# Three pads ahead of and between the operands of TensorE's dense products, in a diffusion layer on one core

## The chip, the cores and the metric

The kernel runs on one core of one Trainium2 chip. Its time is the device time of one execution in microseconds (us); the median of several runs counts. Matrix products run on TensorE (PE), elementwise work on VectorE (DVE) and ScalarE (ACT), a little on GpSimd (POOL); SyncE (SP) issues most of the DMAs. The on-chip memory (SBUF) has 128 partitions. A tile takes a stretch of bytes, the same in every partition, and what this document calls its place or offset is where that stretch begins.

## The reference

One layer of a diffusion backbone over 256 latent tokens and 256 context tokens of width 2048, in float32:

```
h  = modulate(rmsnorm(x), shift, scale)       # also for the context tokens
rw, cv, z, ab, gt = split(h @ w_in)           # one wide input projection
o_a = two-way RWKV-7 scan over heads of rw
o_b = two-way chunked gated DeltaNet of cv, z, ab
m  = sigmoid(g_a) * (o_a @ p_a) + sigmoid(g_b) * (o_b @ p_b)
x  = x + gate1 * (m @ w_out)
f  = modulate(rmsnorm(x), shift2, scale2)
g, u = split(f @ w_gate_up)
x  = x + gate2 * ((silu(g) * u) @ w_down)
out = rmsnorm(x)
```

The FFN's hidden width is 5632. Shifts, scales and gates come from products of the condition vector with w_ada.

## The kernel before, in words

Activations lie with channels on partitions: a tensor of 2048 channels is 16 slices of [128, 256 tokens]. Every dense product is made of three matmuls per slice of 128 input channels. Weights and activations are split into a high part (a copy in the type float32r, made on ScalarE) and a low part (the rest, subtracted on VectorE), and `gemm` (lines 365 to 371) adds hi·hi, hi·lo and lo·hi into one bank of PSUM. The first operand of each matmul is the weights, 128 columns of 512 bytes; the second, the moving operand, is 256 columns (1024 bytes) or 512 (2048 bytes).

The weights come in chunks of up to 8 slices: a DMA loads `wraw` (three buffers), then `whi` and `wlo` (two buffers each) are filled from it. Three places do this: `load_w` (line 340) for the products after the mixers, `low_split` (line 487) for the first stage, and `cast` (line 1025) for the input projection. All of these tiles are in the pool `wp`. `low_split` puts only the even slices there, the odd ones into the pool `p0`.

The work runs in this order.

- To about 130 us: norms, the first part of w_ada, and the low-rank columns of the input projection, in an order written out by hand.
- To about 1390 us: the input projection (moving operands `hxh`, `hxl`, called hx) woven with the two mixers. Here a small planner (`Weave`) gives out the order of TensorE, VectorE, ScalarE and GpSimd by estimated costs. All instructions of this stage go through line 143.
- To about 1490 us: p_a and p_b with the moving operands `oah`, `oal` (oa).
- To about 1590 us: w_out with `mh`, `ml` (m), while the first weights of the FFN are put into a tile of their own, `W4` (its slices are called w in the profile).
- Then the FFN: w_gate_up with `hfh`, `hfl` (hf), and w_down with `za` (the first 32 slices of 128 hidden channels) and `zb` (the last 12).

In the last three steps the order comes from the framework's own schedule, with some instructions held in program order.

Pools are laid from both ends of a partition. From the left: `cst` (constants), `wp` (weights), the pool `arp` with the arena, then the mixers' pool, and in its place later those of m, hf and zb. From the right end: the pool of hx, later those of oa and of W4 and za (`hx`, `gp`, `zap`). Tiles take multiples of 32 bytes.

Of the kernel before, what the change touches and what calls it, by code (L numbers as in the profile page):

```python
# [11 lines left out]
F32 = mybir.dt.float32  # L12
F32R = mybir.dt.float32r
# [5 lines left out]
P = 128  # L19
# [249 lines left out]
def emit(ctx: ExitStack, tc, A, out, dbg=None):  # L269
    nc = tc.nc  # L270
    V, S, G, Q = nc.vector, nc.scalar, nc.gpsimd, nc.sync
# [6 lines left out]
    ent = ctx.enter_context  # L278

    cst = ent(tc.tile_pool(name="cst", bufs=1))  # L280
    wp = ent(tc.tile_pool(name="wp", bufs=2))
    pmm = ent(tc.tile_pool(name="pmm", bufs=3, space=PSUM))
    pa = ent(tc.tile_pool(name="pa", bufs=2, space=PSUM))
    pi = ent(tc.tile_pool(name="pi", bufs=1, space=PSUM))
# [49 lines left out]
    V.memset(scanm.rearrange("p (c t) -> p c t", t=64)[:, :, 0:1], 0.0)  # L334


    wpool, wbufs = [wp], [3, 2, 2]
    wstep = [4]

    def load_w(src, M, nk, kchunk=8, ks=0, into=None):  # L340

        res = []
        pieces = -(-(nk - ks) // kchunk)
        ends = [ks + (nk - ks) * (i + 1) // pieces for i in range(pieces)]
        for k0, k1 in zip([ks] + ends, ends):
            n = k1 - k0
            if into is None:
                raw = wpool[0].tile([P, 8, P], F32, tag="wraw", name="wraw", bufs=wbufs[0])
                hi = wpool[0].tile([P, 8, P], F32R, tag="whi", name="whi", bufs=wbufs[1])
                lo = wpool[0].tile([P, 8, P], F32R, tag="wlo", name="wlo", bufs=wbufs[2])  # L350
            else:
                raw = into[2].tile([P, 8, P], F32, tag="wr", name="wr")
                hi, lo = (t[:, k0:k1] for t in into[:2])
            ld = Q.dma_start(raw[:, :n, :M], src[:, k0:k0 + n, :])
            if into is not None:
                tc.keep_in_program_order(ld)
            for i in range(0, n, wstep[0]):
                c = slice(i, min(i + wstep[0], n))
                S.copy(hi[:, c, :M], raw[:, c, :M])  # L359
                V.tensor_sub(lo[:, c, :M], raw[:, c, :M], hi[:, c, :M].bitcast(F32))  # L360
            for k in range(n):
                res.append((k0 + k, hi[:, k, :M], lo[:, k, :M]))
        return res
# [44 lines left out]
    with tc.tile_pool(name="p0", bufs=1) as p0, \  # L408
# [14 lines left out]
        NL = 736  # L423
# [63 lines left out]
        def low_split(e):  # L487
            res = []
            for k in range(2):
                pool = p0 if e % 2 else wp  # L490
                hi, lo = (pool.tile([P, 8, P] if pool is wp else [P, NL], F32R, tag=f"{t}{k}" if pool is p0 else t, name=t,
                                    bufs=1 if pool is p0 else 2) for t in ("whi", "wlo"))
                if pool is wp:
                    hi, lo = (t.rearrange("p k m -> p (k m)")[:, :NL] for t in (hi, lo))
                S.copy(hi, lws[e][k])
                V.tensor_sub(lo, lws[e][k], hi.bitcast(F32))
                res.append((hi, lo))
            return res
# [10 lines left out]
        for part in range(NE + 1):  # L509
            if part < NE:  # L510
                ps = pst(pmm, "mm")
            for c in range(4):
                if part + 1 < NE:
                    load_ada(part + 1, c)
                if part < NE:
                    ada_part(ps, part, c)
                if c == 0 and part < NE:
                    w = low_split(part)
                    if part + 1 < NE:
                        load_low(part + 1)  # L520
                for _ in itertools.islice(before or (), (0, 1, 2, 1)[c]):
                    pass
            if part < NE:
                rows_of(part, ps, before or ())
                before = low_products(part, w)
            else:
                for _ in before:
                    pass
# [496 lines left out]
    def cast(src, i):  # L1025

        raws = []
        for c in range(2):
            raw = wp.tile([P, 8, P], F32, tag="wraw", name="wraw", bufs=3)
            raws.append((raw, weave.now + dq(raw, src[:, 8 * c:8 * c + 8, :])))  # L1030
        for c, (raw, at) in enumerate(raws):
            if i:
                yield "read", i - 1, c
            yield max(0.0, at - weave.now)
            hi, lo = (wp.tile([P, 8, P], F32R, tag=t, name=t) for t in ("whi", "wlo"))
            for k in range(0, 8, LAT['cg']):
                g = slice(k, k + LAT['cg'])
                yield s.copy(hi[:, g], raw[:, g])
                yield v.tensor_sub(lo[:, g], raw[:, g], hi[:, g].bitcast(F32))
                casts[i, 8 * c + k] = hi, lo  # L1040
                weave.ready("cast", i, 8 * c + k)
# [3 lines left out]
    def products():  # L1045
# [24 lines left out]
        while todo or nxt:  # L1070
            if nxt is None:
                nxt = choose()
                if nxt is None:
                    yield 0.5
                    continue
                if nxt[0] == "g":
                    nxt = "g", next(gate_next)
                weave.add(LAT['crank'], cast(source(*nxt), i))
            what, p = nxt
            nxt = choose()  # L1080
            if nxt is not None:
                if nxt[0] == "g":
                    nxt = "g", next(gate_next)
                weave.add(LAT['crank'], cast(source(*nxt), i + 1))
# [421 lines left out]
    for j in range(KT):  # L1506
        ps = pst(pmm, "mm")
        gemm(ps[:, 0:T], load_w(A["pa"][j], P, 8), Oa, T)
        S.copy(PA[:, j], ps[:, 0:T])
        tc.keep_in_program_order(S.activation(gts[:, 2 * j:2 * j + 2, :], gts[:, 2 * j:2 * j + 2, :], AF.Sigmoid))  # L1510
# [13 lines left out]
    for j in range(KT):  # L1524
        ps = pst(pmm, "mm")
        gemm(ps[:, 0:T], load_w(A["pb"][j], P, 8), Oa, T)
        G.tensor_mul(PA[:, j], PA[:, j], gts[:, j])
        m = x1p.tile([P, T], F32, tag="m", name="m")
        V.tensor_mul(m, ps[:, 0:T], gts[:, 16 + j])
        V.tensor_add(m, m, PA[:, j])  # L1530
        split(M[0][:, j], M[1][:, j], m)
# [6 lines left out]
    for j in range(KT):  # L1538
        ps = pst(pmm, "mm")
        gemm(ps[:, 0:T], load_w(A["wout"][j], P, KT), M, T)  # L1540
        V.scalar_tensor_tensor(x1[:, j, :], ps[:, 0:T], mod[:, 32 + j:33 + j], x1[:, j, :], ALU.mult, ALU.add)
        sq = square_sum(x1p, x1[:, j, :], ssum, j == 0)
        if 0 < j < KT - 1:
            V.tensor_add(ssum, ssum, sq)
        if j % 3 == 2 and j < 12:
            w4.append(load_w(A["wgu"][j // 3], P, KT, into=[W4[:, i, j // 3] for i in range(2)] + [zap]))
# [162 lines left out]
```

## Time and profile before

| | |
|---|---|
| median of 3 runs | 2342.61 us (2338.29 to 2344.66) |
| span of the profiled execution (its first to its last instruction) | 2342.3 us |
| mean granted TensorE clock | 0.972 |
| TensorE busy | 2200.5 us, 94% |
| VectorE busy | 1555.0 us, 66% |
| ScalarE busy | 1101.7 us, 47% |
| moved by DMA | 430.77 MB, mean 184 GB/s |

The profile has no other time of the profiled execution than its span. A group row of the profile reads: line, engine, operation, tile written <- tiles read, shape, count | busy us, mean ns of one | idle time before it and what ended that. A timeline row begins with the start and the length in us. A stage row has the stage, its length, the busy time and count of PE, weight loads (PEld), DVE, ACT and POOL, then the granted clock, the share of the DMA engines and GB/s. The length of a matmul is modelled and overlaps that of the next one, so the pace of a row of matmuls is read from their starts.

### The profile page before, as it was taken

Reading aid. Unit: us, or ns where it says so; the run is one execution under the profiler, and the core shown is the slowest. Engines: PE = TensorE matmul, PEld = TensorE weight load, DVE = VectorE, ACT = ScalarE, POOL = GpSimd, SP = SyncE. Lnnn points to the kernel's source line nnn. Section 1 sums busy time; section 2 is a strip of 40 time slices with the busy share of each in tenths; the row PEclk is TensorE's granted clock in tenths of the full one; section 3 lists DMA queues with packets and bytes.
Section 4 is the critical chain, followed back from the end, with each engine's and each line's share of the span. In section 5 each row is a group of like instructions: output and inputs, shape, how many; then the busy total and the mean of one; then the engine's idle time right before and its main releaser. Section 6 shows DMA issues by size and latency. Waiting matters only on the chain.

```text
span 2342.3 us, 54751 instructions
## 1 busy us (share of the span) xinstructions
PE 2200.5 (94%) x22904; PEld 1940.9 (83%) x22904; DVE 1555.0 (66%) x3238; ACT 1101.7 (47%) x2058; POOL 110.6 (5%) x183
## 2 busy tenths in 40 slices
PE   7989999999999999888888999999999999999998
PEld 4767677787777778666677989999999999999997
DVE  3447588888877568889788745765565655555554
ACT  3246454454455555454455546544444444444443
POOL 0000000000000011111111003000000000000000
PEclk9999999999999899989899999999999999999999
DMA  9956543443443237556566665563777766556665
GB/s 380 397 149 187 159 113 96 118 116 97 112 117 109 89 125 229 176 175 193 160 199 212 194 220 189 205 219 117 234 233 232 237 236 215 188 189 191 192 192 164
DMA packets 232727, 430.77 MB, mean 184 GB/s; under 512 B 114848, under 2 KB 130208, under 8 KB 228128
## 3 DMA queue, kind: packets, MB, share of 16 engines
q1 hardware_dynamic: 204832, 351.77, 47.3%
q0 software_dynamic: 13824, 50.34, 6.8%
q10 hardware_dynamic: 13824, 25.17, 3.3%
q8 instruction: 179, 2.93, 0.5%
q14 instruction: 68, 0.56, 0.1%
HBM read 401.44 MB, written 25.77 MB: 182 GB/s over the span
## 4 chain that ended last, share of the span: by engine, by line
PE 62%; DVE 11%; DMA 6%; ACT 4%; issue 2%; SPq 0%; ACTq 0%; DVEq 0%
PE mm L143 16%; PE mm L371 12%; PE mm L369 12%; PE mm L370 12%; PE s L143 4%; DVE arena L143 4%; PE pa L143 3%; PE pi L143 2%; DVE aw L143 2%; DVE wlo L143 2%; DMA wr<-wgu 1%; DMA tscr<-arena 1%; ACT arena L143 1%; DMA Tx<-tscr 1%; DVE wlo L360 1%
## 5 line engine op out<-in xcount | busy, mean ns | idle before, releaser
L360 DVE TENSOR_TENSOR wlo<-wraw,whi 128x1024 fp32r<-128x1024 f32 x328 | 393.0, 1199 | 348.8 <-ACT whi L359 345.7
L359 ACT CAST whi<-wraw 128x1024 fp32r<-128x1024 f32 x328 | 337.6, 1030 | 472.2 <-PE mm L370 427.9
L143 PE MATMUL mm<-hxh,wlo 128*128 128x256 f32 (+1 forms) x1376 | 471.0, 342 | 11.7 <-DVE wlo L143 11.3
L143 PE MATMUL mm<-hxh,whi 128*128 128x256 f32 (+1 forms) x1376 | 470.8, 342 | 8.7 <-ACT whi L143 7.3
L143 PE MATMUL mm<-hxl,whi 128*128 128x256 f32 (+1 forms) x1376 | 464.7, 338 | 0.0
L371 PE MATMUL mm<-hfh,wlo 128*128 128x256 f32 x1344 | 376.6, 280 | 0.6 <-DVE wlo L360 0.6
L369 PE MATMUL mm<-hfh,whi 128*128 128x256 f32 x1344 | 375.8, 280 | 0.0
L370 PE MATMUL mm<-hfl,whi 128*128 128x256 f32 x1344 | 374.7, 279 | 0.0
L143 PEld LDWEIGHTS mm<-hxh,wlo 128*128 128x128 f32 x1376 | 266.1, 193 | 42.4 <-DVE wlo L143 16.4
L143 PEld LDWEIGHTS mm<-hxh,whi 128*128 128x128 f32 x1376 | 266.8, 194 | 36.2 <-ACT whi L143 10.8
L143 PEld LDWEIGHTS mm<-hxl,whi 128*128 128x128 f32 x1376 | 266.5, 194 | 26.3 <-issue 5.7
L143 DVE TENSOR_TENSOR wlo<-wraw,whi 128x512 fp32r<-128x512 f32 x344 | 236.0, 690 | 68.3 <-ACT whi L143 66.7
L371 PEld LDWEIGHTS mm<-hfh,wlo 128*128 128x128 f32 x1344 | 252.6, 188 | 1.1 <-DVE wlo L360 1.0
L369 PEld LDWEIGHTS mm<-hfh,whi 128*128 128x128 f32 x1344 | 252.8, 188 | 0.0
L370 PEld LDWEIGHTS mm<-hfl,whi 128*128 128x128 f32 x1344 | 252.8, 188 | 0.0
L143 ACT CAST whi<-wraw 128x512 fp32r<-128x512 f32 x344 | 205.8, 617 | 98.7 <-PE mm L143 63.0
L369 PE MATMUL mm<-za,whi 128*128 128x256 f32 x512 | 141.6, 277 | 0.0
L371 PE MATMUL mm<-za,wlo 128*128 128x256 f32 x512 | 141.4, 276 | 0.0
L370 PE MATMUL mm<-za,whi 128*128 128x256 f32 x512 | 141.4, 276 | 0.0
L143 DVE TENSOR_TENSOR arena<-arena 128x39 f32<-128x39 f32 (+17 forms) x522 | 120.9, 234 | 23.8 <-DMA arena<-scr 8.0
L143 DVE SCALAR_TENSOR_TENSOR aw<-aw,ck 128x512 f32<-128x512 f32 x180 | 132.6, 750 | 6.0 <-DMA aw<-ada_rest 5.8
L370 PEld LDWEIGHTS mm<-za,whi 128*128 128x128 f32 x512 | 96.1, 188 | 0.0
(329 smaller groups left out, 3926.5 us busy)
## 6 DMA issues: line engine op xcount, KB each, us to landing
wraw<-w SPq DMA_DIRECT2D x172, 512.0 KB, 4.0
wraw<-wgu SPq DMA_DIRECT2D x168, 512.0 KB, 4.4
aw<-ada_rest POOLq DMA_DIRECT2D x96, 512.0 KB, 4.6
aw<-ada_first SPq DMA_DIRECT2D x32, 1024.0 KB, 11.7
wraw<-wdn SPq DMA_DIRECT2D x64, 448.0 KB, 3.5
wraw<-wout SPq DMA_DIRECT2D x32, 512.0 KB, 4.2
aw<-ada_gt ACTq DMA_DIRECT2D x64, 256.0 KB, 4.8
wraw<-wdn SPq DMA_DIRECT2D x32, 512.0 KB, 3.5
```

The source lines that it names most:

```text
L143: return Op(self, cost, lambda: getattr(self.engine, name)(out, *a, **k), split)
L359: S.copy(hi[:, c, :M], raw[:, c, :M])
L360: V.tensor_sub(lo[:, c, :M], raw[:, c, :M], hi[:, c, :M].bitcast(F32))
L369: E.matmul(ps, hi, Xh[:, k, :n], start=first and i == 0, stop=False)
L370: E.matmul(ps, hi, Xl[:, k, :n], start=False, stop=False)
L371: E.matmul(ps, lo, Xh[:, k, :n], start=False, stop=last and i == len(wt) - 1)
```

## The change

Three pads are added; no operation on data is changed. A tile `rpad` of 32 bytes is laid at the right end, ahead of the pools there. A tile `lpad` of 32 bytes is laid in `cst` after `scanm` (a mask), and so ahead of a few small constants and of `wp`. The tiles `whi` and `wlo` of `wp` get 16 numbers (64 bytes) behind their 8 slices, by a new helper that all three places call. Two small fills on VectorE write the first two pads.

```
@@ emit
     wp = ent(tc.tile_pool(name="wp", bufs=2))
+    rpad = ent(tc.tile_pool(name="rpad", bufs=1, side="right")).tile([P, 8], F32, name="rpad")
...
     V.memset(scanm.rearrange("p (c t) -> p c t", t=64)[:, :, 0:1], 0.0)
+    lpad = cst.tile([P, 8], F32, name="lpad")
+    V.memset(lpad, 0.0)
+    V.memset(rpad, 0.0)
+    def split_tile(tag, bufs=2):
+        return wp.tile([P, 8 * P + 16], F32R, tag=tag, name=tag, bufs=bufs)[:, :8 * P].rearrange("p (k m) -> p k m", k=8)
@@ load_w
-                hi = wpool[0].tile([P, 8, P], F32R, tag="whi", name="whi", bufs=wbufs[1])
-                lo = wpool[0].tile([P, 8, P], F32R, tag="wlo", name="wlo", bufs=wbufs[2])
+                hi, lo = split_tile("whi"), split_tile("wlo")
@@ low_split
-                hi, lo = (pool.tile([P, 8, P] if pool is wp else [P, NL], F32R, tag=f"{t}{k}" if pool is p0 else t, name=t,
-                                    bufs=1 if pool is p0 else 2) for t in ("whi", "wlo"))
-                if pool is wp:
-                    hi, lo = (t.rearrange("p k m -> p (k m)")[:, :NL] for t in (hi, lo))
+                hi, lo = (split_tile(t).rearrange("p k m -> p (k m)")[:, :NL] if pool is wp else
+                          p0.tile([P, NL], F32R, tag=f"{t}{k}", name=t) for t in ("whi", "wlo"))
@@ cast
-            hi, lo = (wp.tile([P, 8, P], F32R, tag=t, name=t) for t in ("whi", "wlo"))
+            hi, lo = (split_tile(t) for t in ("whi", "wlo"))
```

## The prediction

> **What bounds the kernel now.** I read the page's busy shares and its clock row first, then the chain that ended last, then the busy time by stage, then the groups of matmuls by form, and at last the starts of single matmuls. The first view shows TensorE (PE) busy for 94% of the span, far above the next engine; the chain names dense products (lines 369 to 371, and the "mm" products of line 143) for half of the path; the stages show where nothing but their pace counts.
>
> ```profile
> span 2342.3 us, 54751 instructions
> PE 2200.5 (94%) x22904; PEld 1940.9 (83%) x22904; DVE 1555.0 (66%) x3238; ACT 1101.7 (47%) x2058; POOL 110.6 (5%) x183
> by line: PE mm L143 16.1%; PE mm L371 12.2%; PE mm L369 12.1%; PE mm L370 12.1%; PE s L143 4.1%; DVE arena L143 3.9%; PE pa L143 3.2%; issue 2.1%; PE pi L143 2.1%; DVE aw L143 1.9%; DVE wlo L143 1.7%; DMA wr<-wgu 1.1%; DMA tscr<-arena 1.1%;
> 0.00:130.00 130.00, 113.56 (x1338) 81.07 (x1339) 54.27 (x147) 37.56 (x71) 0.41 (x5) 0.97 0.96 365
> 130.00:1390.00 1260.00, 1157.76 (x13691) 936.00 (x13690) 965.25 (x2378) 636.01 (x1432) 88.84 (x162) 0.96 0.51 150
> 1620.00:2087.00 467.00, 466.40 (x3980) 465.91 (x3979) 270.69 (x380) 198.52 (x248) 0.00 (x0) 1.00 0.66 221
> 2088.00:2325.00 237.00, 237.00 (x2071) 236.78 (x2070) 119.38 (x125) 106.27 (x127) 0.00 (x0) 1.00 0.64 190
> ```
>
> From 1620 us on PE never idles at a granted clock of 1.00, while VectorE is busy for 58% and the DMA engines for 64 to 66%. There a nanosecond per matmul is a nanosecond of the result. From 130 to 1390 us only part counts. The first 130 us are DMA-bound (share 0.96).
>
> The counts of the terms are those of the groups:
>
> ```profile
> L371 PE MATMUL mm<-hfh,wlo 128*128 128x256 f32 x1344 | 376.6, 280 | 0.6 <-DVE wlo L360 0.6
> L143 PE MATMUL mm<-hxl,whi 128*128 128x256 f32 x880 | 255.1, 290 | 0.0
> L143 PE MATMUL mm<-hxl,whi 128*128 128x512 f32 x496 | 209.6, 423 | 0.0
> L370 PE MATMUL mm<-za,whi 128*128 128x256 f32 x512 | 141.4, 276 | 0.0
> L371 PE MATMUL mm<-oah,wlo 128*128 128x256 f32 x256 | 71.9, 284 | 0.5 <-DVE wlo L360 0.5
> L371 PE MATMUL mm<-mh,wlo 128*128 128x256 f32 x256 | 72.7, 284 | 4.0 <-DVE wlo L360 4.0
> L371 PE MATMUL mm<-zb,wlo 128*128 128x256 f32 x192 | 53.8, 280 | 0.0
> ```
>
> Each row is one of three equal groups (hi·hi, hi·lo, lo·hi). Their "mean" is a modelled length, so the pace has to be taken from starts. These rows of the timeline are the first and the last of undisturbed stretches:
>
> ```profile
> 2105.11 0.28 PE L370 MATMUL mm<-za,whi 128*128 128x256 f32 x1
> 2111.91 0.28 PE L370 MATMUL mm<-za,whi 128*128 128x256 f32 x1
> ...
> 1430.02 0.28 PE L371 MATMUL mm<-oah,wlo 128*128 128x256 f32 x1
> 1437.09 0.28 PE L371 MATMUL mm<-oah,wlo 128*128 128x256 f32 x1
> ...
> 1655.01 0.28 PE L369 MATMUL mm<-hfh,whi 128*128 128x256 f32 x1
> 1690.01 0.28 PE L369 MATMUL mm<-hfh,whi 128*128 128x256 f32 x1
> 1850.03 0.28 PE L371 MATMUL mm<-hfh,wlo 128*128 128x256 f32 x1
> 1885.36 0.28 PE L371 MATMUL mm<-hfh,wlo 128*128 128x256 f32 x1
> ...
> 177.71 0.28 PE L143 MATMUL mm<-hxh,whi 128*128 128x256 f32 x1
> 180.21 0.28 PE L143 MATMUL mm<-hxl,whi 128*128 128x256 f32 x1
> 146.05 0.28 PE L143 MATMUL mm<-hxh,wlo 128*128 128x256 f32 x1
> 148.53 0.28 PE L143 MATMUL mm<-hxh,wlo 128*128 128x256 f32 x1
> ...
> 153.91 0.39 PE L143 MATMUL mm<-hxh,whi 128*128 128x512 f32 x1
> 159.18 0.39 PE L143 MATMUL mm<-hxh,wlo 128*128 128x512 f32 x1
> ```
>
> Start to start, at full clock and with the same shape: za 6.80 us over 60 matmuls, 113.3 ns; oa 7.07 over 60, 117.8; hf 35.00 over 300, 116.7, and after a stall at 1772 us 35.33 over 300, 117.8; hx 2.50 over 22, 113.6, but 2.48 over 21, 118, in most of its stretches (216 of some 1,700 undisturbed triples of starts are fast, hence a mean of 117.2). At 512 columns 5.27 over 23, 229. So the same product has several steady paces, 4% apart, which hold for tens of microseconds and change at a stall.
>
> Do places decide? I worked the byte offset of each tile in a partition out of the tile sizes, in the order in which the pools lay them, and took it modulo 128. The slices that a matmul reads are 512 or 1024 bytes apart, so one number tells a whole product. Before: the weights whi, wlo 32, all four buffers; the right-hand operands (hx, oa, za) 96; the left-hand ones (hf, m, zb) 64. The right-hand ones show a constant 113.3 or 117.8; the left-hand ones 116.7 or 117.8 and no 113.3. So place matters, but it is no full cause: oa and za share their offsets and differ by 4.5 ns.
>
> **The change part by part.** rpad takes 32 bytes at the right end: hx, oa, za go from 96 to 64. lpad takes 32 bytes ahead of the weights, and each of the four whi/wlo buffers grows by 64: the weights go from 32 to 64 (buffer 0) and 0 (buffer 1), which alternate by chunk of up to 8 slices. Everything laid after them moves by 32+4·64 = 288: hf, m, zb go from 64 to 96, the arena from 32 to 64.
>
> The two fills (memset) run on VectorE at the start, before it waits 3 us for a load; a fill of 8 numbers cost 65 ns, so they are hidden, and 0.13 us without that cover.
>
> ```profile
> L334 DVE MEMSET scanm<- 128x8 bf16 x1 | 0.1, 65 | 0.1
> 4.57 0.18 DVE L325 TENSOR_SCALAR om<-PR 128x29 f32<-128x29 f32 x1 [3.01 <-DMA PR<-prm]
> L496 DVE TENSOR_TENSOR wlo<-wraw,whi x16: 914/916/925, 29.1 to 114.3; 128x736 fp32r<-128x736 f32 x16
> L495 ACT CAST whi<-wraw x16: 787/800/806, 28.3 to 113.1; 128x736 fp32r<-128x736 f32 x16
> ```
>
> VectorE and ScalarE: in the first stage even slices are split into tiles at 32 and odd ones at 64, and the 16 splits lie within 914 to 925 and 787 to 806 ns. I take nothing; 1% either way stays beside PE. No DMA is added or moved in a queue, and no wait is added; wraw moves from 32 to 64, the first stage's aw from 64 to 96. No row prices an offset for DMAs, and I take 0 between -1 and +1 us in the DMA-bound first stage; later they have a third of their time in hand.
>
> That leaves the pace of TensorE. The row nearest to the new left-hand pairing (weights 64, moving 96) is an odd slice of the first stage:
>
> ```profile
> 131.92 0.28 PE L369 MATMUL pa<-hxh,whi 128*128 128x256 f32 x1
> 132.51 0.28 PE L371 MATMUL pa<-hxh,wlo 128*128 128x256 f32 x1
> 1598.49 0.28 PE L371 MATMUL mm<-hfh,w 128*128 128x256 f32 x1
> 1609.26 0.28 PE L369 MATMUL mm<-hfh,w 128*128 128x256 f32 x1
> 1593.01 0.41 PE L369 MATMUL mm<-hfh,whi 128*128 128x256 f32 x1
> 1593.87 0.41 PE L370 MATMUL mm<-hfl,w 128*128 128x256 f32 x1
> ```
>
> 0.59 us over 5 matmuls, 118.2 ns. Steps in us:
> - hf, m, zb, 3·(1344+256+192) = 5376 matmuls, 117.1 now (the two hf rows by their time; 192 matmuls with w are left out). Chunks with weights at 64: +1.1·2688 = +3.0. Chunks with weights at 0: no row; ends 113.3 (-10.2) and 118.2 (+3.0). Nearest by offset is again 118.2, but it comes from five matmuls without a settled cycle; I take the fast end, as a bet: -10.2. Together -7.2.
> - oa, 768: weights and moving now both start on a multiple of 64 bytes, where a slice spans 8 and 16 pieces of 64 bytes and not 9 and 17. Ends 0 and -4.45·0.768 = -3.4; I take -3.4.
> - za, 1536: stays at 113.3, 0; the other end is oa's pace, +6.8.
> - hx, 256 columns, 2640: 117.2 to 113.3 is -10.3, at 512 columns, 1488: some 230.7 (the mean over undisturbed starts) to 229 is -2.5. Of this stage's dense time, 2640·0.117+1488·0.231 = 653 us, the chain holds 16.1%, 377 us, so 0.58 of it counts: -7.4.
> Sum -18.0, from 2342.3 to 2324.3. The span is 0.3 us under the median of the runs, 2342.6, so no correction is made. Late next, as PE gets faster, is the split's write of wlo; its waits in the left-hand rows above are under 1 us in 1344, so it keeps up.
>
> [...]
>
> **The rivals.**
> - Only the relation of weights to moving operand counts, and modulo 64 it is the same before and after (0 on the right, 32 on the left). Then the same paces are drawn anew. For it: oa and za. Against it: the w4 rows below. Price between -3.4 (oa) and +6.8 (za): 2342. [...]
> - No short cycle is kept. The weights' offset now changes with each chunk, so the pattern is upset every 24 matmuls. For it: where hf met weights of four tiles in turn (w, from 1598.49), 10.77 us over 91 matmuls, 118.3. Against it: the offsets were constant there too. Price at 118.3 throughout: left 1.2·5376 = +6.5, za +7.6, oa +0.4, hx 1.1·2640·0.58 = +1.7: 2358.5. It decides (over 7 us) as soon as za alone falls to 118.
> - The stall goes altogether. At half clock a matmul takes 0.86/4 = 0.215 us, which is its 256 columns with next to no stall; half of that is 107. At 107: left 10.1·5376 = -54, za -9.7, oa -8.3, hx -16 and at 512 columns 17·1488·0.58 = -15: 2239. Against it: no stretch comes under 113. [...]
>
> **How the numbers follow.** The forecast with its neighbours (part of the groups fast) has 0.46, 2311 (all products at 113.3) to 2335; the stall gone 0.04; paces drawn anew 0.20; no short cycle 0.30, 2349 to 2358. Nothing under 0.3%, 7 us, can be told from no change. Faster 0.50, same 0.20, slower 0.30. The range, 2306 to 2356, leaves out the stall gone, the last edge of the slow case and little else; with the DMA bound it would be 1 us wider. The faster case alone has 2306 to 2335.
>
> **What would show it.** Right: oa and hx at 113.3 start to start, za unchanged, hf under 116. Wrong for the right side: oa still 117.8. Wrong for the left: hf at 118 in both kinds of chunks. The chunks tell buffer 0 from buffer 1. The prediction falls if za leaves 113.3, or if the splits or the first 130 us change by more than 1%.

## The result, and the profile after

The changed kernel is slower: 2353.93 us median against 2342.96 for the kernel before, a ratio of 1.0043 with a 95% interval of 1.0027 to 1.0059. The forecast was 2324 us. The time lies in the range given, the direction does not.

The page of the changed kernel (its first lines), and its busy time by stage in the columns shown before:

```profile
span 2355.0 us, 54753 instructions
PE 2214.3 (94%) x22904; PEld 1953.0 (83%) x22904; DVE 1555.4 (66%) x3240; ACT 1101.1 (47%) x2058; POOL 110.5 (5%) x183
```

```profile
0.00:130.00 130.00, 114.30 (x1336) 81.42 (x1337) 54.32 (x149) 37.58 (x71) 0.41 (x5) 0.97 0.97 365
130.00:1390.00 1260.00, 1157.08 (x13683) 933.26 (x13681) 963.60 (x2373) 633.70 (x1426) 88.80 (x162) 0.96 0.51 150
1620.00:2087.00 467.00, 466.73 (x3935) 466.36 (x3934) 267.55 (x376) 196.36 (x247) 0.00 (x0) 1.00 0.67 219
2088.00:2325.00 237.00, 237.00 (x2019) 237.00 (x2019) 116.00 (x122) 103.26 (x123) 0.00 (x0) 1.00 0.64 186
```

The span is 12.7 us longer. The work is the same (22,904 matmuls, the two added fills on VectorE). The granted clock is the same in the FFN rows, PE still never idles there, but fewer matmuls start in the same stretch: 3935 for 3980 from 1620 us on, 2019 for 2071 from 2088 us on. The same matmuls follow one another more slowly.

Where it was lost shows in the starts of the stages on PE, first before, then after (timeline; start, length, instruction):

```profile
1387.57 0.80 PE L369 MATMUL mm<-oah,whi 128*128 128x256 f32 x2 [3.54 <-ACT oah L374]
1488.60 0.28 PE L369 MATMUL mm<-mh,whi 128*128 128x256 f32 x1
1589.96 0.50 PE L369 MATMUL mm<-hfh,w 128*128 128x256 f32 x2 [2.07 <-ACT hfh L1558]
2087.86 0.28 PE L369 MATMUL mm<-za,whi 128*128 128x256 f32 x1
```

```profile
1389.94 0.79 PE L377 MATMUL mm<-oah,whi 128*128 128x256 f32 x2 [3.62 <-ACT oah L382]
1490.14 0.29 PE L377 MATMUL mm<-mh,whi 128*128 128x256 f32 x1
1591.42 0.50 PE L377 MATMUL mm<-hfh,w 128*128 128x256 f32 x2 [2.07 <-ACT hfh L1564]
2094.46 0.27 PE L377 MATMUL mm<-za,whi 128*128 128x256 f32 x1
```

Up to oa +2.4 us; oa 101.0 to 100.2, -0.8; m 101.4 to 101.3, -0.1; hf 497.9 to 503.0, +5.1; from za to the end of the span 254.4 to 260.5, +6.1. Together 12.7, half of it in the last stage, where the prediction held za at no change. Experiments 9 and 11 below are one kernel profiled twice: up to oa its two executions differ by 4.1 us, in each later stage by 0.9 at most. So the +2.4 up to oa can't be told from chance, the +5.1 and the +6.1 can.

The paces behind it, by starts again (the columns of the timeline). In turn: a chunk of oa with its weights at 64 and the settled part of one with its weights at 0, eight columns of hf, and one column of the last stage (96 matmuls of za and 36 of zb):

```profile
1456.42 0.28 PE L377 MATMUL mm<-oah,whi 128*128 128x256 f32 x1
1459.28 0.29 PE L377 MATMUL mm<-oah,whi 128*128 128x256 f32 x1
1460.22 0.28 PE L379 MATMUL mm<-oah,wlo 128*128 128x256 f32 x1
1461.92 0.28 PE L379 MATMUL mm<-oah,wlo 128*128 128x256 f32 x1
...
1650.32 0.28 PE L377 MATMUL mm<-hfh,whi 128*128 128x256 f32 x1
1695.81 0.28 PE L377 MATMUL mm<-hfh,whi 128*128 128x256 f32 x1
...
2109.97 0.27 PE L377 MATMUL mm<-za,whi 128*128 128x256 f32 x1
2125.47 0.27 PE L377 MATMUL mm<-za,whi 128*128 128x256 f32 x1
```

oa: 2.86 us over 24 is 119.3 ns with the weights at 64, 1.70 over 15 is 113.3 with the weights at 0. hf: 45.49 over 384 is 118.5 (before 116.7 or 117.8). The last stage: 15.50 over 132 is 117.5. The two kinds of chunks in oa differ by 6 ns and alternate; za shows nearly the same two paces, 119.2 and 114.6 over whole chunks. Here and below, the settled part of a chunk is what follows its first six matmuls.

Three of the groups by form, as the page of before had them, show the same from another side (busy us, modelled mean ns | idle before):

```profile
L379 PE MATMUL mm<-hfh,wlo 128*128 128x256 f32 x1344 | 378.8, 282 | 0.3 <-DVE wlo L368 0.3
L378 PE MATMUL mm<-za,whi 128*128 128x256 f32 x512 | 143.3, 280 | 0.0
L379 PE MATMUL mm<-mh,wlo 128*128 128x256 f32 x256 | 73.2, 286 | 3.1 <-DVE wlo L368 3.1
```

Busy time is 2.2 us more in the first and 1.9 in the second, with no more idle time ahead of them: 0.3 us for 0.6, and none. In m it is 0.5 us more, and the wait for wlo is 0.9 us less: there the splits set part of the time, and the slower matmuls are hidden behind them.

The other parts of the change cost what was said. One of the two fills, and the splits of the first stage with their weights elsewhere:

```profile
L339 DVE MEMSET lpad<- 128x8 f32 x1 | 0.1, 65 | 0.0
```

```profile
L502 DVE TENSOR_TENSOR wlo<-wraw,whi x16: 912/917/925, 29.3 to 114.8; 128x736 fp32r<-128x736 f32 x16
L501 ACT CAST whi<-wraw x16: 788/799/808, 28.5 to 113.6; 128x736 fp32r<-128x736 f32 x16
```

917 for 916 ns and 799 for 800: these splits don't feel the moved starts.

### The profile page after: what moved, and what is told of

It is laid out like the page before. It is cut to its first block, busy times and chain, and to the rows that moved or that the text cites. A ratio compares the mean times of both kernels' runs of the same rounds, so it can differ in the third digit from the quotient of the medians.

```text
span 2355.0 us, 54753 instructions
## 1 busy us (share of the span) xinstructions
PE 2214.3 (94%) x22904; PEld 1953.0 (83%) x22904; DVE 1555.4 (66%) x3240; ACT 1101.1 (47%) x2058; POOL 110.5 (5%) x183
## 4 chain that ended last, share of the span: by engine, by line
PE 63%; DVE 11%; DMA 5%; ACT 4%; issue 2%; SPq 1%; DVEq 0%; ACTq 0%; POOL 0%
PE mm L143 16%; PE mm L379 13%; PE mm L377 13%; PE mm L378 12%; PE s L143 4%; DVE arena L143 4%; PE pa L143 3%; DVE aw L143 2%; PE pi L143 2%; DVE wlo L143 2%; DMA tscr<-arena 1%; ACT arena L143 1%; DMA wr<-wgu 1%; DMA arena<-scr 1%; DMA Tx<-tscr 1%
## 5 line engine op out<-in xcount | busy, mean ns | idle before, releaser
L143 DVE TENSOR_TENSOR arena<-arena 128x39 f32<-128x39 f32 (+17 forms) x522 | 121.2, 234 | 20.8 <-ACT arena L143 6.3
L379 PEld LDWEIGHTS mm<-za,wlo 128*128 128x128 f32 x512 | 96.6, 189 | 0.0
```

The source lines that it names most:

```text
L143: return Op(self, cost, lambda: getattr(self.engine, name)(out, *a, **k), split)
L379: E.matmul(ps, lo, Xh[:, k, :n], start=False, stop=last and i == len(wt) - 1)
```

## The experiments

One number orders what follows: the **difference**, the offset of the weights minus that of the moving operand, modulo 128 bytes. In these kernels it is:

| kernel | left (hf, m, zb) | right (hx, oa, za) |
|---|---|---|
| before | 96 | 64 |
| after, buffer 0 / buffer 1 | 96 / 32 | 0 / 64 |

In the expectations, theory P says that a pair of places has a pace of its own, as read off the chunks of the changed kernel, whatever comes before; theory R that the places count by their difference alone; theory A that it is the change of offset from chunk to chunk that costs. A "column" is one column of 128 outputs. All paces are means of start-to-start times in ns, at full clock and, where nothing else is said, at 256 columns. All kernels here compute everything.

**1. The pad behind whi and wlo taken away.** lpad and rpad stay; the difference no longer alternates: left 96, right 0.

```
-        return wp.tile([P, 8 * P + 16], F32R, ...
+        return wp.tile([P, 8 * P], F32R, ...
```

> lpad and rpad stay, the 64 bytes behind whi and wlo go: all weights at 64 (offsets modulo 128), right-hand operands at 64, left-hand at 96, and nothing alternates between chunks. Theory P (each pairing of offsets has its own pace, whatever came before): the changed kernel's chunks with weights at 64 settled at 119.1 ns on the right and 118.9 on the left, and now all are such chunks: against before left 1.8 x 5376 = +9.7 us, za 5.6 x 1536 = +8.6, oa 1.3 x 768 = +1.0, hx about +4: some 2366 us, slower than the changed kernel. Theory A (the change of offset from chunk to chunk upsets the cycle and costs the time): 113 to 118 ns as before, 2335 to 2350 us.

Measured: 2351.35 us, ratio 1.0055 (1.0036 to 1.0075). Rows of its timeline, hf and then za:

```profile
1686.37 0.28 PE L377 MATMUL mm<-hfh,whi 128*128 128x256 f32 x1
1697.57 0.28 PE L377 MATMUL mm<-hfh,whi 128*128 128x256 f32 x1
...
2117.00 0.28 PE L378 MATMUL mm<-za,whi 128*128 128x256 f32 x1
2127.08 0.28 PE L378 MATMUL mm<-za,whi 128*128 128x256 f32 x1
```

za: 10.08 us over 84, 120.0 ns. A difference of 0 is among the slowest met, and it is this kernel's loss. hf: 11.20 over 96, 116.7, its pace of before, with weights (64) and moving operand (96) where the changed kernel settles at 118.7 in such chunks. So P falls on the left: what a pair of places gives depends on whether the difference holds or alternates. Theory A alone, with 2335 to 2350 us, doesn't do either: nothing alternates here, and za is slower than in the changed kernel.

**2. A difference of 64 everywhere, held.** Weights at 0, all moving operands at 64.

```
+    mpad = ent(tc.tile_pool(name="mpad", bufs=1)).tile([P, 8], F32, name="mpad")
-    lpad = cst.tile([P, 8], F32, name="lpad")
+    lpad = cst.tile([P, 24], F32, name="lpad")
-        return wp.tile([P, 8 * P + 16], F32R, ...
+        return wp.tile([P, 8 * P], F32R, ...
```

> lpad of 96 bytes, no pad behind whi and wlo, 32 bytes behind the weights, rpad of 32: all weights at 0, all moving operands, left and right, at 64. Theory P: in the changed kernel right-hand chunks of this pairing settled at 113.4 ns (oa, za) and 114 (hx); so left -3.7 x 5376 = -19.9 us, oa -4.4 x 768 = -3.4, za 0, hx -3.2 x 2640 x 0.58 = -4.9 against before, some 2315 us. Theory A: a paired pace drawn anew between 113 and 118, 2322 to 2350 us.

Measured: 2340.64 us, ratio 0.9993 (0.9975 to 1.0010). hf:

```profile
1639.99 0.28 PE L379 MATMUL mm<-hfh,whi 128*128 128x256 f32 x1
1662.60 0.28 PE L379 MATMUL mm<-hfh,whi 128*128 128x256 f32 x1
```

22.61 us over 192, 117.8 ns, and za the same, while 64% of the settled matmuls of oa ran at 113.3. So 64 has shown two steady paces, 113.3 and 117.8, and hf and za kept the one that they had entered. P's 2315 us took the first for the only one; the range of theory A holds the time.

**3. The pad behind whi and wlo alone.** No lpad, no rpad: weights at 32 and 96, right 96, left 64. No place is that of the changed kernel; every difference is.

```
-    rpad = ent(tc.tile_pool(name="rpad", bufs=1, side="right")).tile([P, 8], F32, name="rpad")
-    lpad = cst.tile([P, 8], F32, name="lpad")
-    V.memset(lpad, 0.0)
-    V.memset(rpad, 0.0)
```

> Only the 64 bytes behind whi and wlo, neither lpad nor rpad: weights at 32 and 96, right-hand operands at 96, left-hand at 64; modulo 128 weights minus moving operand are as in the changed kernel, with everything 32 bytes lower. Theory R (only the difference counts): the changed kernel's paces chunk by chunk (right 119 where the difference is 0, 113.4 where it is 64), 2354 us. Theory A gives the same time. Theory P in its wide form (both offsets count): other paces; with 118.3 at (96,64), 117 at (32,64), and 113.3 to 117.8 at (32,96), 2340 to 2354 us.

Measured: 2353.62 us, ratio 1.0063 (1.0039 to 1.0086). hf, then the last stage:

```profile
1660.05 0.28 PE L374 MATMUL mm<-hfl,whi 128*128 128x256 f32 x1
1705.70 0.28 PE L374 MATMUL mm<-hfl,whi 128*128 128x256 f32 x1
...
2156.92 0.28 PE L373 MATMUL mm<-za,whi 128*128 128x256 f32 x1
2187.72 0.28 PE L373 MATMUL mm<-za,whi 128*128 128x256 f32 x1
```

hf 45.65 us over 384, 118.9; the last stage 30.80 over 264, 116.7. By kind of chunk, za settles at 113.3 with a difference of 64 and at 118.8 with 0 (113.4 and 119.1 in the changed kernel), hf has, over the whole stage and within chunks, 118.5 with 32 and with 96 (118.4 with both in the changed kernel). That is theory R, with one exception: oa settles at 116.4 in its chunks of 64, where the changed kernel has 113.8. So nearly the same paces come with other places at the same differences, and the 64 bytes behind whi and wlo alone bring the whole loss. lpad and rpad beside them leave the left's differences as they are and swap those of the right between the buffers, and the time is the same.

**4. Only the left-hand operands moved.** A pad behind the weights puts them from 64 to 96; weights 32 and right 96 stay as before. Difference 64 everywhere.

```
+    mpad = ent(tc.tile_pool(name="mpad", bufs=1)).tile([P, 8], F32, name="mpad")
(no lpad, no rpad, no pad behind whi and wlo)
```

> Only 32 bytes behind the weights, no other pad: weights at 32, all moving operands at 96, the pairing that the kernel before has on the right alone. Theory R (difference 64): left-hand products settle at 113.4 ns as the right-hand chunks of difference 64 do in the changed kernel, -19.9 us, about 2323 us. Theory P: left-hand products take one of the two paces that this pairing showed before, 113.3 (2323 us) or 117.8 (2347 us), and may change at a stall.

Measured: 2347.54 us, ratio 1.0022 (1.0001 to 1.0043). The last stage:

```profile
2099.74 0.28 PE L375 MATMUL mm<-za,whi 128*128 128x256 f32 x1
2130.83 0.28 PE L375 MATMUL mm<-za,whi 128*128 128x256 f32 x1
```

31.09 us over 264, 117.8 ns. The places of za are those of the kernel before, where it had 113.3. So even a product that isn't touched changes its pace, and theory R's 2323 us, with 113.4 for every difference of 64, fails. What fits is that the state in which a product is entered, left by the work ahead of it, chooses between the two. That is an inference from the paces: no trace shows such a state, and with one profile of each kernel, that the choice differs from execution to execution isn't ruled out.

**5. A sweep.** 128 bytes behind whi and wlo, and in the FFN the slices start 0, 4, 8 ... 124 bytes into their tiles, a different offset for each column of w_gate_up.

```
+    woff = [0]
...
-        return wp.tile([P, 8 * P + 16], ...)[:, :8 * P]
+        o = woff[0]
+        return wp.tile([P, 8 * P + 32], ...)[:, o:o + 8 * P]
...
+                woff[0] = (j - 2) % 32      (w_gate_up, column j)
+            woff[0] = 2 * j                 (w_down, column j)
```

> A look, not a comparison of times: the weights' slices start a varying number of floats into their tiles, o = 0 to 31 over the 42 later column pairs of the FFN's first product, and 0, 2, ... 30 over the 16 columns of its second. Offset of weights minus moving operand, modulo 128 bytes: 4o-32 for hf, 8j-64 for za, 8j-32 for zb. Theory R (the difference modulo 128 sets which paces exist): where it is 0, 120 ns as in the run without the pad behind whi and wlo; at 96, 116.7 or 117.8; at 64, 113.3 or 117.8; at 32, 118.3; za and zb agree with hf at equal difference. What lies between these is not known; if only pieces of 32 bytes count, the map has four steps. If the place in itself counts (theory P), za and zb disagree with hf at equal difference.

Measured: 2352.48 us in one execution. The pace of hf by difference, in ns (two values: the two products of the column differ):

```
  0 119.0        4 118.4/119.4   8 117.0       12 116.7
 16 117.4       20 118.0        24 118.9/119.5 28 118.3
 32 119.3       36 118.6        40 119.7       44 118.4
 48 118.0       52 113.3        56 117.8       60 118.7/119.1
 64 117.8/113.3 68 118.0        72 117.8       76 113.3
 80 117.6       84 118.4        88 117.0       92 120.1/119.4
 96 117.5/117.1 100 119.7      104 117.7/118.9 108 119.9
112 119.6/118.6 116 119.4      120 118.6      124 119.1
```

Rows of its timeline for 52 and 76:

```profile
1854.95 0.28 PE L376 MATMUL mm<-hfh,whi 128*128 128x256 f32 x1
1860.39 0.28 PE L376 MATMUL mm<-hfh,whi 128*128 128x256 f32 x1
...
1919.49 0.28 PE L378 MATMUL mm<-hfh,wlo 128*128 128x256 f32 x1
1922.21 0.28 PE L378 MATMUL mm<-hfh,wlo 128*128 128x256 f32 x1
```

5.44 us over 48 and 2.72 over 24, 113.3 ns each. The pace changes from one step of 4 bytes to the next, and of the ten differences that the sweep meets twice nine gave the same settled paces, product by product, within 0.2 ns; 96 did not. Of 32 differences, 52 and 76 alone were fast in both products. Theory R had named 120 for a difference of 0 and 118.3 for 32: the sweep has 119.0 and 119.3. za, in chunks of other lengths, mostly had other paces at the same difference, which the expectation held to be a sign of theory P. With several paces to a difference it needn't be one, but the sweep doesn't decide it: this is a map of what hf falls into, not of all that a difference allows.

**6. 128 bytes behind whi and wlo.** Another pitch, no place changed modulo 128.

```
-        return wp.tile([P, 8 * P + 16], F32R, ...
+        return wp.tile([P, 8 * P + 32], F32R, ...
(no lpad, no rpad)
```

> 128 bytes behind whi and wlo in place of 64, no lpad and no rpad: the buffers lie 4224 bytes apart and modulo 128 all offsets are those of before. Theory R: the paces of before (hf 116.7 or 117.8, oa and za 113.3 or 117.8), 2335 to 2350 us, and none of the 118.5 to 119 of the changed kernel. If it is the pitch of the buffers that costs, and not the offset modulo 128, 2354 us.

Measured: 2338.17 us, ratio 0.9992 (0.9966 to 1.0018). The pad as such costs nothing that can be told. The paces are not quite those of before: oa has 113.8 on the mean for 117.8, and hf goes from chunk to chunk between 116.5 and 117.4, where the kernel before held one pace from stall to stall. So the same places modulo 128 gave oa nearly its fast pace without any move, and whether 128 bytes is the whole measure isn't shown.

**7. A difference of 32 everywhere, held.** Weights at 96, all moving operands at 64.

```
+    mpad = ent(tc.tile_pool(name="mpad", bufs=1)).tile([P, 16], F32, name="mpad")
-    lpad = cst.tile([P, 8], F32, name="lpad")
+    lpad = cst.tile([P, 16], F32, name="lpad")
-        return wp.tile([P, 8 * P + 16], F32R, ...
+        return wp.tile([P, 8 * P], F32R, ...
```

> lpad of 64 bytes, 64 behind the weights, rpad of 32, nothing behind whi and wlo: weights at 96, all moving operands at 64, difference 32 throughout, nothing alternates. Theory R with a pace for each difference: 118.3 to 118.5 everywhere (the first weights of the FFN before, and the changed kernel's left-hand chunks with weights at 0), so left +1.3 x 5376 = +7 us, za +7.6, oa +0.4, hx +1.7 against before: some 2359 us. Theory A (alternation costs by itself and 118.5 is its price): 117 to 118, 2343 to 2350 us.

Measured: 2363.03 us, ratio 1.0086 (1.0051 to 1.0122), the slowest of all. hf:

```profile
1670.34 0.28 PE L379 MATMUL mm<-hfh,whi 128*128 128x256 f32 x1
1704.90 0.28 PE L379 MATMUL mm<-hfh,whi 128*128 128x256 f32 x1
```

34.56 us over 288, 120.0 ns; oa and za 118.3. So 32 is slow without any alternation (theory A had 2343 to 2350 us), and no product ran near 113 there.

The first products of hf, with the weights w, are a case of their own: w lies in a tile that no pad alternates, and its difference changes from kernel to kernel. In the changed kernel it went from 32 to 96:

```profile
1601.07 0.28 PE L377 MATMUL mm<-hfh,w 128*128 128x256 f32 x1
1615.07 0.28 PE L377 MATMUL mm<-hfh,w 128*128 128x256 f32 x1
```

14.00 us over 120, 116.7 ns, where the prediction's rows from 1598.49 us on had 118.3: the only product on the left that became faster. Experiments 3 and 6 (difference 32) have 118.3 and 118.4, experiment 1 (96) has 116.6. At a difference of 0 there are two values, and they go with the place: 118.7 with both starts at 64 (experiments 2 and 7), 119.8 to 120.0 with both at 96 (4, 8 to 12). So the difference tells most, but that the places drop out altogether is not shown.

**8, 9 and 10. The two fast differences, held and in turn.** The slices start 12 bytes into their tiles (difference 76 everywhere), 116 bytes (52), or 12 and 116 from chunk to chunk. A pad of 32 bytes behind the weights (mpad) puts the left at 96, where the right is.

```
-        return wp.tile([P, 8 * P + 16], ...)[:, :8 * P]
+        return wp.tile([P, 8 * P + 32], ...)[:, 3:3 + 8 * P]       (8; in 9: 29:29 + 8 * P)
...
+        splits[tag] = splits.get(tag, 0) + 1                       (10)
+        o = (3, 29)[splits[tag] % 2]
+        return wp.tile([P, 8 * P + 32], ...)[:, o:o + 8 * P]
```

> Weights start at 44 and all moving operands at 96 (modulo 128 bytes): a difference of 76 in every dense product, without alternation. The sweep had 113.3 ns in hf at that difference, in both halves of a column. If that pace belongs to the difference (theory R) and it is the only steady one there: hf, m and zb at 113.3 (5376 matmuls, 3.8 ns less: -20 us), oa and za at 113.3, hx at 113.3 to 114 (-5 us), some 2314 us. If the difference has several steady paces of which the sweep showed one: hf, za at 116 to 118, 2335 to 2348 us.

> Weights start at 20 and all moving operands at 96: a difference of 52 everywhere, where the sweep had 113.3 ns in hf as well. Same as for 76: 2314 us if 113.3 is the only steady pace at this difference, 2335 to 2348 us if it is one of several. If 52 and 76 come out apart from each other, 113.3 in the sweep was chance in one of them.

> The slices of whi and wlo start 12 or 116 bytes into their tiles, in turn from chunk to chunk: differences of 76 and 52 in alternate chunks. If alternation itself costs (the short cycle is upset every 24 matmuls and not found again): hf 118 to 119, za 117, some 2350 us or more. If only the paces that belong to the two differences count, and a chunk enters its own within a few matmuls: hf and za at 113.3 to 115, 2314 to 2325 us, as fast as with either difference alone.

Measured: 76 held 2329.09 us, ratio 0.9923 (0.9891 to 0.9955); 52 held 2322.70, ratio 0.9899 (0.9856 to 0.9941); in turn 2340.93, the median of ten executions between 2318 and 2364 (the ratio, 0.9972 with 0.9931 to 1.0013, is of the eight up to 2352), while its profiled one has a span of 2324.5. Rows of hf, from 76 and then from the alternating kernel:

```profile
1690.04 0.28 PE L376 MATMUL mm<-hfl,whi 128*128 128x256 f32 x1
1706.36 0.28 PE L376 MATMUL mm<-hfl,whi 128*128 128x256 f32 x1
```

```profile
1661.60 0.28 PE L378 MATMUL mm<-hfh,whi 128*128 128x256 f32 x1
1694.24 0.28 PE L378 MATMUL mm<-hfh,whi 128*128 128x256 f32 x1
```

16.32 us over 144 and 32.64 over 288, 113.3 ns each; hf, za and zb have it in 96% or more of their settled matmuls in all three. The two differences kept on these products what the sweep showed on hf. Not on all: oa has 114.2 to 114.7 on the mean, hx at 256 columns 115.7 to 116.9 (117.3 before), which is part of why the times stay above the 2314 us expected. And in the profiled execution alternation between them costs nothing: not one matmul of those 288, in 12 chunks, is late. What the slower executions of the alternating kernel did no profile shows; their spread, 46 us for 16 and 6 with one difference held, says that it doesn't always fall so well.

**11 and 12. The difference 52 again, and 52 in turn with 96.** The second has `o = (8, 29)[...]`.

> The kernel with the difference 52 everywhere, once more, for a closer interval. If its paces belong to the difference, dense products at 113.3 ns again and some 2323 us, 0.8% under the kernel before; if the first result was a lucky draw, 2335 to 2345 us.

> Differences of 52 and 96 in alternate chunks, in every dense product. If a chunk goes by its own difference whatever came before, hf has 113.3 in the chunks with 52 and 116.7 or 117.8 in those with 96, which are its paces where it stands alone. If the change of difference itself costs where the difference has several paces, the chunks with 96 show 118.8 to 119.3, as in the changed kernel, and those with 52 113.3 to 114. About 2335 us in the first case and 2340 in the second.

Measured: 52 held 2323.12 us, ratio 0.9899 (0.9870 to 0.9928); 52 and 96 in turn 2357.88 in one execution. Here are rows of the alternating kernel: the chunk of hf with difference 52, in one column and in the next:

```profile
1667.57 0.28 PE L378 MATMUL mm<-hfh,whi 128*128 128x256 f32 x1
1670.31 0.28 PE L378 MATMUL mm<-hfh,whi 128*128 128x256 f32 x1
1673.20 0.28 PE L378 MATMUL mm<-hfh,whi 128*128 128x256 f32 x1
1676.08 0.28 PE L378 MATMUL mm<-hfh,whi 128*128 128x256 f32 x1
```

2.74 us over 24, 114.2 ns (113.3 after six matmuls), and 2.88 over 24, 120.0: the same buffers, moving operand and difference, and the two columns go on in turn like this. The first follows a chunk of 96 that repeats 120, 116, 117, 119, 122, the second one of 96 at a constant 120. The chunks of 96 settle at 119.3 on the mean in hf, for 116.7 where 96 is held. So neither expectation was right for 52, which has a slow pace too, and the second was right for 96. What fits all this, again as an inference, is that a chunk falls into one of the paces of its difference by the state in which the chunk before leaves PE. Where the difference is held, one pace mostly stays until a stall: between its stalls at 1620, 1772 and 1953 us hf before has 116.7 in every chunk and then 117.7 to 117.8.

## Why the prediction was wrong

What held: PE's pace in the dense products is what moves the time; the fills, VectorE, ScalarE and the DMAs cost nothing that can be told (the DMA share of the first stage is 0.97 for 0.96); the splits keep up as before. oa's fast half and za's fall to 118, named as what would decide, could be read off the chunks as said.

What failed, step by step:

- **The measure of place.** This is the step that failed first. The prediction gave each operand its own place and took the pace from the row with the nearest places, and from whether both start on a multiple of 64. Experiment 3 has the differences of the changed kernel with none of its places, and nearly all its paces; experiment 5 has another pace at most steps of 4 bytes. Modulo 64 the left side before (96) and the new chunks of buffer 1 (32) are one class; on the chip they are 116.7 and 118.3 to 120. The rival "only the relation counts" had the right quantity, with the wrong modulus, and for that reason the wrong time, 2342.
- **Left, chunks with the weights at 0: a bet on 113.3, -10.2 us.** They have 118.4. By difference there was a row in the prediction itself: hf with the weights w at 96 and the operand at 64, difference 32, 118.3 ns. It was read as what four tiles in turn do to a cycle. Experiment 7 holds 32 and has 120.0: the difference itself is slow.
- **Left, chunks with the weights at 64: 118.2 from five matmuls, +3.0.** The size was near (118.4 over whole chunks of hf, 118.7 settled), the reason was not: 96 is the difference of before, and gives 116.7 when held (experiment 1). It is the change of difference every 24 matmuls that costs here. hf, m and zb together came out at about +1.5 ns over 5376 matmuls, +8 us, for the -7.2 forecast; in m the wait for the splits hid it.
- **za stays at 113.3, 0.** This is the largest single miss after the bet. Half of its chunks went to a difference of 0, which has 119 in alternation and 120 held (experiment 1); the stage lost 6.1 us, by the paces of single matmuls 5.7 of it in za (113.5 to 117.2 over 1536). The other end, +6.8, was the right one. That za had kept 113.3 was no property of its place in any case: experiment 4 leaves its places alone, and it has 117.8.
- **oa to 113.3, -3.4.** Right in the chunks with difference 64 (113.3 after six matmuls), wrong in those with 0 (119.3): 117.1 on the mean, and -0.8 us for the stage. The reason, the multiples of 64, isn't shown, so the right half is luck: experiment 6, with the places of before, has 113.8 in oa.
- **hx, -7.4.** Its chunks at difference 64 settle at 114.4, those at 0 at 119.3; together 117.7 for 117.3. The time to oa is 2.4 us longer, which is within what two executions of one kernel differ by there.

The rival "no short cycle is kept" had the direction, the two largest terms (left +6.5 by its 118.3, za +7.6) and 2358.5 us, against 2353.93 measured. Its mechanism is half of the truth: the chunks of 32 and 0 are slow by their difference, held or not, and only those of 96 lose a cycle that they would have. Nor did alternation upset anything in the profiled execution of experiment 10; its slower executions stay unexplained.

That every place is a multiple of 32 bytes does not fix the time either: so it is in the kernels before, after and 1 to 4 and 7, and their times lie between 2340.64 and 2363.03 us.

The rival "the stall goes altogether" is not met: its 107 ns, half of the pace at half clock, shows nowhere, and the fastest steady pace in thirteen kernels is 113.3. What it started from can be read in the trace of before. At a granted clock of 0.50 matmuls at 512 columns follow one another at 427 ns (2.56 us over 6), twice the 0.215 us of 256 columns:

```profile
171.76 0.63 PE L143 MATMUL mm<-hxh,wlo 128*128 128x512 f32 x1
174.32 0.59 PE L143 MATMUL mm<-hxh,wlo 128*128 128x512 f32 x1
```

**A faster kernel.** With the difference at 52 in all products but those with w, the kernel takes 2323 us in both series, 1.0% under the kernel before. Its stages say where. In experiment 9 oa starts at 1384.51 us, m at 1482.94, hf at 1583.95 and za at 2069.44, with a span of 2321.5. Against before that is -3.1 us up to oa, -2.6 in oa, -0.4 in m, -12.4 in hf and -2.4 from za on, together -20.8. So most of it is hf, at 113.4 ns for 117.1; the part up to oa is no gain that can be told (the second profile, experiment 11, has +1.1 there). The time is near the one that the prediction gave, by way of a pace which this change did not bring.

## What to carry to other kernels

When PE never idles and the same matmul shows several steady paces, work out the start of the weights minus that of the moving operand modulo 128 bytes for each product, and compare rows by that number before calling one "nearest". It is a hint and not a law: equal differences gave unequal paces here too (113.3 and 117.8 at 64). Then sweep it on the chip in steps of the element, in one kernel, and hold the best value in all buffers: a pad that shifts one of two alternating buffers gives the product two differences in turn, and each chunk follows one with the other difference. A pace that a product shows once isn't its own until it has come back after a stall, or in a second kernel.

## What the runs showed of the hardware that was not expected

- The same 128x128 by 128x256 matmul runs at steady paces between 113.3 ns (za before) and 120.0 (hf in experiment 7), 6% apart. In these runs the paces went with where the operands start, and mostly by the difference of the two starts alone: of the ten differences that the sweep meets twice, nine gave the same settled paces within 0.2 ns, but in hf with w a difference of 0 had 118.7 with both starts at 64 and 119.8 to 120.0 with both at 96. Steps of 4 bytes matter: in the sweep 48, 52 and 56 have 118.0, 113.3 and 117.8.
- A steady pace is here a repeated cycle of start-to-start times. The trace of before has three of them: 113, 113, 114 ns in za (113.3), 120, 113, 116, 117 in hf from 1640 us on (116.7), mostly 119, 116, 118 in hf from 1775 us on (117.8), each to within 2 ns. Several differences have more than one: 64 has 113.3 (za before) and 117.8 (oa before), 96 has 116.7 and 117.8 (hf before), 118.8 and 120 (experiment 12), 52 has 113.3 and, entered from a chunk at a constant 120, 120.0 (experiment 12). The differences 52 and 76 come back to 113.3 by themselves after most stalls in hf, za and zb (96% or more of the settled matmuls in experiments 8 to 10), 64 often doesn't (117.8 in oa before and in hf in experiment 2).
- At 512 columns the difference doesn't order the paces: 52 and 76, the fastest at 256, have 233.0 and 232.5 ns there (the kernels of experiments 9 and 8) for 230.5 before, but the difference of before, 64, itself has 230.5 (experiment 4), 231.8 (6) and 232.9 (2).
- Why these cycles exist, and what the memory does in them, no run here shows.
